# Queueing the weight casts of six gated-unit tiles behind a sigmoid, and two sets of operand combinations behind two low parts, in a bidirectional encoder layer

## The chip, the cores and the metric

The kernel runs on one core of one Trainium2 chip. The metric is the time of one execution on the device in microseconds; the figure given for a kernel is the median of its runs. The core has five engines with a queue of instructions each: TensorE (PE, matrix products into eight PSUM banks), the Vector engine (DVE), the Scalar engine (ACT), GpSimd (POOL) and SyncE (SP), which here issues most of the DMA transfers. An engine takes its instructions in the order of its queue; between engines, semaphores carry the dependences.

## What is computed

One layer of a hybrid encoder on 1024 positions of width 1024, in float32: a normalisation, one wide projection, two parallel mixers (a gated convolution module and a bidirectional linear recurrence), a merge, and a gated feed-forward block. The change touches only the beginning: the gated linear unit that feeds the convolution.

```python
h = _rmsnorm(x, attn_norm_w[layer])
proj = jnp.einsum("bsd,de->bse", h, w_in)
glu_in, q, v, z_f, z_b, og, g_a, g_b = jnp.split(proj, SPLIT_POINTS, axis=-1)
a = jax.nn.glu(glu_in, axis=-1)          # first half * sigmoid(second half), 512 columns each
a = _dwconv_centred(a, dw_w, dw_b)       # 31 taps over positions
```

## The kernel before

**Products in three parts.** Every operand of a product is split into a high part (a rounded copy, made by ACT) and a low part (source minus high part, made by DVE); `split` at L123 issues the two, both recorded at L124. `mm3` (L143) then makes one product of float32 accuracy from three matmuls: high by high (L148), high by low (L149), low by high (L150). PE's matmuls of one 128-column tile over 512 positions (one *half*) are 8 x 3 = 24.

**Tiles of the gated unit.** There are four column groups j, each with a *gate* tile (columns 512 + 128j) and a *value* tile (columns 128j), in two halves of 512 positions. `evac_b` (L848) takes a finished gate half out of its bank with a sigmoid (L851, on ACT) into a page of the tag "tm"; `evac_a` (L855) multiplies the value half by that page into `gl` (L857, on DVE). Both use the PSUM tag "mm", which has three banks. `glu_jobs` (L916) gives the order: a first job for j = 0, then first halves, both halves of j = 3, and last the second halves of gate 0, value 0, gate 1, value 1, gate 2, value 2. These are the "last six tiles" of the change.

**Preparing ahead.** `std_job` (L250) is a pair: `prep` loads the tile's 512 KB of raw weights (`raw_w`, L133, tag "wr", two pages, the DMA issued on SP at L135) and splits them into two of four "wp" pages; `run` issues the matmuls in pieces, four for a half. `run_jobs` (L194) calls the `prep` of a tile as the tile before it starts. A tile's weight pages are those of the tile two before it.

**Operand combinations.** After the gated unit the projections go through pairs of columns by a scheme with seven products instead of eight (`pair_job`, L282, first built as `pair0`). It needs differences of quadrants of h. `h_combos` (L937) loads three quadrants for each k = 0..3 into the tag "su" (four pages, L944 on SP), and `combos` (L461) makes three differences (L466, on DVE; the first of them into a "tm" page, of which there are four) and splits each into pages "hy" (L124 on ACT and DVE).

**What sets the order.** PE's order is written by hand: `Stream.fill(n)` advances the stream of the gated unit by n pieces, and `s_glu.fill(GLU_LATE)` with GLU_LATE = 17 stands behind the call of `h_combos` (L966, L967). PE does nothing in `h_combos`. The orders of ACT, DVE, POOL and SP are made when the program is built, by a scheduler that models the execution and ranks each instruction by how late it may be issued; the order in which instructions are traced in the program is one of its inputs. `tc.issue_after(i)` adds to this: what the block traces on the engine of `i` is issued behind `i`, without waiting for it to finish. Once built, an order is fixed.

After the gated unit the convolution follows (`conv_steps`, L1028): 31 steps on DVE for each j (L1036, L1039), with pieces of the pairs in between.

Of the kernel before, what the change touches and what calls it, by code (L numbers as in the profile page):

```python
# [10 lines left out]
F32 = mybir.dt.float32  # L11
# [3 lines left out]
AF = mybir.ActivationFunctionType  # L15
ALU = mybir.AluOpType
AX = mybir.AxisListType

P = 128
# [10 lines left out]
GLU_LATE = 17  # L30
# [17 lines left out]
def tile_hybrid_encoder(  # L48
# [24 lines left out]
    V, A, G, T = nc.vector, nc.scalar, nc.gpsimd, nc.tensor  # L73

    S, D = x.shape[1], x.shape[2]
    ND = D // P
    CW = conv_dw_w.shape[2]
# [16 lines left out]
    def nm(s):  # L94
        uid[0] += 1
        return f"{s}_{uid[0]}"
# [3 lines left out]
    def bank(tag):  # L100
        return ps.tile([P, H], F32, tag=tag, name=nm(tag), bufs=BANKS[tag])

    def page(pool, tag, bufs, dt=F32):
        return pool.tile([P, H], dt, tag=tag, name=nm(tag), bufs=bufs)

    def tmp():
        return page(mp, "tm", 4)
# [15 lines left out]
    def split(hi, lo, src, eng, late=False):  # L123
        parts = A.copy(hi, src), eng.tensor_tensor(lo, src, hi.bitcast(F32), op=ALU.subtract)  # L124
        if late:
            for i in parts:
                pin(i)
        return hi, lo

    def w_cols(w, r0, nk, c0, cols=P):  # L130
        return w[0, r0 : r0 + nk * P, c0 : c0 + cols].rearrange("(k p) e -> p k e", p=P)

    def raw_w(src, nk):  # L133
        t = mp.tile([P, nk, P], F32, tag="wr", name=nm("wr"), bufs=2)
        nc.sync.dma_start(t, src)  # L135
        return t

    def w_page(nk, pool=None):
        if pool is None:
            return mp.tile([P, nk, P], F32R, tag="wp", name=nm("wp"), bufs=4)  # L140
        return pool.tile([P, nk, P], F32R, tag="wq", name=nm("wq"), bufs=3)

    def mm3(acc, w, act, k, first, last, again=False):  # L143


        whi, wlo = w
        ahi, alo = act
        T.matmul(acc, whi[:, k, :], ahi, start=first, stop=False, skip_group_check=again)  # L148
        T.matmul(acc, whi[:, k, :], alo, start=False, stop=False, skip_group_check=again)  # L149
        T.matmul(acc, wlo[:, k, :], ahi, start=False, stop=last, skip_group_check=again)  # L150
# [43 lines left out]
    def run_jobs(jobs, lead=0, prime=0, first=None):  # L194


        live = collections.deque(maxlen=3)

        jobs = jobs if isinstance(jobs, collections.deque) else collections.deque(jobs)
        ready = collections.deque()  # L200

        def prepare(n):
            while jobs and len(ready) < n:
                prep, run = jobs.popleft()
                ready.append((run, prep()))
                live.append(ready[-1][1])

        def tick():
            for w in live:
                if isinstance(w, Weights):  # L210
                    w.tick()
            advance_chores()

        prepare(max(prime, 1))
        if prime:
            yield
        while ready:
            run, w = ready.popleft()
            pieces = run(w)
            for _ in itertools.islice(pieces, lead if first is None else first):  # L220
                tick()
                yield
            first = None
            prepare(1)
            for _ in pieces:
                tick()
                yield
            prepare(1)
# [21 lines left out]
    def std_job(src, nk, acts, evac, halves=(0, 1), step=2):  # L250


        def prep():
            raw = raw_w(src, nk)
            return split(w_page(nk), w_page(nk), raw, V)

        def run(w, halves=halves):
            for half in halves:
                acc = bank("mm")
                for k in range(nk):  # L260
                    mm3(acc, w, acts(k, half), k, k == 0, k == nk - 1)
                    if k % step == step - 1 or k == nk - 1:
                        yield
                evac(half, acc)

        return prep, run
# [194 lines left out]
    def combos(ops, k, b11, b12, b22, alloc):  # L461

        def sub(o, a, b):
            V.tensor_tensor(o, a, b, op=ALU.subtract)  # L466

        def parts(i, src):
            ops[i].append(split(alloc(), alloc(), src, V))

        t3 = page(mp, "tm", 4)
        sub(t3, b12, b22)
        parts(7, t3)
        sub(b22, t3, b11)
        parts(6, b22)
        sub(b12, b11, b12)
        parts(5, b12)
# [104 lines left out]
    def in_cols(c0):  # L582
        return w_cols(w_in, 0, ND, c0)
# [3 lines left out]
    ht = {i: [] for i in range(1, 8)}  # L587
# [256 lines left out]

    gate = {}
    early = []

    def evac_b(j):  # L848
        def evac(hf, acc):
            gate[j, hf] = tmp()  # L850
            A.activation(gate[j, hf], acc, AF.Sigmoid)  # L851

        return evac

    def evac_a(j):  # L855
        def evac(hf, acc):
            V.tensor_tensor(  # L857
                gl[j][:, PAD + hf * H : PAD + (hf + 1) * H], acc, gate.pop((j, hf)), op=ALU.mult
            )

        return evac

    def glu_tiles(j, halves):
        yield std_job(in_cols(CW + j * P), ND, h_std, evac_b(j), halves)
        yield std_job(in_cols(j * P), ND, h_std, evac_a(j), halves)

    glu_raw, glu_w = [], []

# [6 lines left out]
    def glu_first():  # L875


        def prep():
            for _ in range(2):
                glu_raw.append(mp.tile([P, ND, P], F32, tag="wr", name=nm("wr"), bufs=2))  # L880
                glu_w.append((w_page(ND), w_page(ND)))
            for g in range(2):
                ks = slice(g * NK2, (g + 1) * NK2)
                for c, raw in zip((CW, 0), glu_raw):
                    nc.sync.dma_start(raw[:, ks], in_cols(c)[:, ks])

        def run(_):
            accs = [bank("mm"), bank("mm")]
            seen = [0, 0]

            def mm(n, k, wp, ap):
                w, a = glu_w[n][wp][:, k, :], h_std(k, 0)[ap]
                seen[n] += 1
                T.matmul(accs[n], w, a, start=seen[n] == 1, stop=seen[n] == 3 * ND)


            mm(0, 0, 0, 0)
            mm(0, 0, 1, 0)
            yield
            mm(0, 1, 0, 0)  # L900
            mm(0, 1, 1, 0)
            for n, wp, ap in ((0, 0, 1), (1, 0, 0), (1, 0, 1), (1, 1, 0)):
                for k in range(2):
                    mm(n, k, wp, ap)
            yield
            for k in range(2, ND):
                for n in range(2):
                    for wp, ap in ((0, 0), (1, 0), (0, 1)):
                        mm(n, k, wp, ap)
                yield  # L910
            evac_b(0)(0, accs[0])
            evac_a(0)(0, accs[1])

        return prep, run

    def glu_jobs():  # L916
        def loaded(job, key, pages):
            def prep():
                return split(pages(), pages(), early[key], V)

            return prep, job[1]

        def early_page():
            return p0.tile([P, ND, P], F32R, tag="xn", name=nm("wp"), bufs=4)

        yield glu_first()
        job0, job1 = glu_tiles(1, (0,))
        yield loaded(job0, 0, early_page)
        yield loaded(job1, 1, lambda: w_page(ND))
        job0, job1 = glu_tiles(2, (0,))  # L930
        yield loaded(job0, 2, lambda: w_page(ND))
        yield job1
        yield from glu_tiles(3, (0, 1))
        for j in (0, 1, 2):
            yield from glu_tiles(j, (1,))

    def h_combos():  # L937
        def hy():
            return page(p1, "hy", 24, F32R)

        for k in range(NK2):
            b11, b12, b22 = (page(p1, "su", 4) for _ in range(3))
            for t, (kk, half) in ((b11, (k, 0)), (b12, (k, 1)), (b22, (k + NK2, 1))):
                nc.sync.dma_start(t, d_h[kk][half])  # L944
            combos(ht, k, b11, b12, b22, hy)

    s_glu = Stream(run_jobs(glu_jobs(), prime=1, first=GLU_LEAD))
    s_glu.fill()
    ahead = p0.tile([P, ND, P], F32, name="ahead")
# [13 lines left out]
    s_glu.fill(GLU_MORE)  # L963
    p0.release()
    p1 = tc.alloc_tile_pool(name="p1", bufs=1, reuse_waits="tile")
    h_combos()  # L966
    s_glu.fill(GLU_LATE)  # L967
    pair0 = in_pair(0)
    w_pair0 = pair0[0]()
    s_glu.drain()  # L970
# [737 lines left out]
    for k in range(NK2):  # L1708
        s_out.fill(16 if k else 17) if k < NK2 - 1 else s_out.drain()
        b11, b12, b21, b22 = x2[k][0], x2[k][1], x2[k + NK2][0], x2[k + NK2][1]  # L1710
# [358 lines left out]
```

## Time and profile before

| | |
|---|---|
| median of 3 runs | 1721.52 us (1721.14 to 1722.52) |
| the profiled execution | 1721.94 us, span 1720.0 us |
| PE busy | 99% of the span |
| DVE, ACT, POOL busy | 73%, 48%, 14% |
| mean granted PE clock | 0.998 |

In a row of a timeline stand the start in the span, the length in us, the engine, the line in the kernel, the operation with output and inputs, shapes and how many instructions are merged; in brackets the idle time of that engine before it, and what ended it. PE rows are matmuls whose ends are modelled, so the distance between starts says more than the lengths. "SPq" rows are the issue of transfers. In a view by windows stand the stretch, then for PE, weight loads (PEld), DVE, ACT and POOL the busy time and the count, then the granted PE clock, the share of the DMA engines and GB/s. A row of waits gives who waited for whom, the total, the number of times and the longest.

### The profile page before, as it was taken

Reading aid. Unit: us, or ns where it says so; the run is one execution under the profiler, and the core shown is the slowest. Engines: PE = TensorE matmul, PEld = TensorE weight load, DVE = VectorE, ACT = ScalarE, POOL = GpSimd, SP = SyncE. Lnnn points to the kernel's source line nnn. Section 1 sums busy time; section 2 is a strip of 40 time slices with the busy share of each in tenths; the row PEclk is TensorE's granted clock in tenths of the full one; section 3 lists DMA queues with packets and bytes.
Section 4 is the critical chain, followed back from the end, with each engine's and each line's share of the span. In section 5 each row is a group of like instructions: output and inputs, shape, how many; then the busy total and the mean of one; then the engine's idle time right before and its main releaser. Section 6 shows DMA issues by size and latency. Waiting matters only on the chain.

```text
span 1720.0 us, 30762 instructions
## 1 busy us (share of the span) xinstructions
PE 1699.1 (99%) x11902; PEld 1416.2 (82%) x11902; DVE 1256.6 (73%) x1937; ACT 825.0 (48%) x1544; POOL 240.7 (14%) x281
## 2 busy tenths in 40 slices
PE   8999999999999999999999999999999999999998
PEld 6878888788788888888888888888888888888787
DVE  4599999745779888888656466667777776657865
ACT  6443443233577777776442245444434433542334
POOL 1212222200001111111100002122222222000110
PEclk9999999999999999999999999999999999999999
DMA  8777888854673444435689466577778776783842
GB/s 281 238 181 177 201 191 189 203 160 148 202 261 91 146 127 133 128 116 200 223 277 279 143 205 199 147 159 153 165 166 174 171 172 154 229 266 102 215 95 99
DMA packets 337096, 308.28 MB, mean 179 GB/s; under 512 B 17582, under 2 KB 249142, under 8 KB 336950
## 3 DMA queue, kind: packets, MB, share of 16 engines
q1 hardware_dynamic: 289590, 267.51, 49.1%
q0 software_dynamic: 47360, 38.81, 15.5%
q8 instruction: 93, 1.52, 0.4%
q14 instruction: 53, 0.43, 0.1%
HBM read 201.40 MB, written 87.03 MB: 168 GB/s over the span
## 4 chain that ended last, share of the span: by engine, by line
PE 61%; DVE 1%; ACT 1%; DMA 0%; issue 0%; POOLq 0%; ACTq 0%; SPq 0%; DVEq 0%
PE mm L148 14%; PE mm L150 14%; PE mm L149 14%; PE sc L148 3%; PE sc L150 3%; PE sc L149 3%; PE ob L1375 2%; PE tr L148 1%; PE tr L150 1%; PE tr L149 1%; PE sc L1197 1%; PE sc L1283 1%; PE mm L1334 1%; PE sc L1334 1%; PE ob L1197 0%
## 5 line engine op out<-in xcount | busy, mean ns | idle before, releaser
L148 PE MATMUL mm<-hx,wp 128*128 128x512 f32 x1068 | 426.9, 400 | 2.3 <-ACT tm L851 1.4
L150 PE MATMUL mm<-hx,wp 128*128 128x512 f32 x1068 | 416.9, 390 | 0.5 <-DVE wp L124 0.5
L149 PE MATMUL mm<-hx,wp 128*128 128x512 f32 x1068 | 416.2, 390 | 0.0
L124 ACT CAST wp<-wr 128x1024 fp32r<-128x1024 f32 (+2 forms) x147 | 147.3, 1003 | 217.8 <-PE mm L149 180.3
L148 PEld LDWEIGHTS mm<-hx,wp 128*128 128x128 f32 x1068 | 200.6, 188 | 45.0 <-DVE ev L800 2.2
L150 PEld LDWEIGHTS mm<-hx,wp 128*128 128x128 f32 x1068 | 200.5, 188 | 44.4 <-DVE wp L124 1.6
L149 PEld LDWEIGHTS mm<-hx,wp 128*128 128x128 f32 x1068 | 200.8, 188 | 39.2 <-issue 0.7
L124 DVE TENSOR_TENSOR wp<-wr,wp 128x1024 fp32r<-128x1024 f32 (+2 forms) x145 | 169.1, 1167 | 39.1 <-ACT wp L124 32.7
L1039 DVE SCALAR_TENSOR_TENSOR acc<-gl,v_b,acc 128x1024 f32<-128x1024 f32 x120 | 148.7, 1272 | 0.4
L440 ACT COPY su<-mm 128x512 f32<-128x512 f32 x82 | 47.7, 582 | 80.1 <-PE mm L150 80.1
L1315 POOL DMA_DIRECT2D S<-D x64 | 36.3, 573 | 284.2 <-ACT S L1313 155.6
L1144 DVE TENSOR_TENSOR qF<-qF,tb 128x512 f32<-128x512 f32 x96 | 65.5, 684 | 13.3 <-ACT A L1178 12.7
L124 ACT CAST wq<-sw 128x1024 fp32r<-128x1024 f32 x41 | 43.2, 1053 | 61.2 <-PE mm L149 32.9
L148 PE MATMUL tr<-hx,wp 128*128 128x512 f32 x180 | 70.5, 392 | 0.0
L150 PE MATMUL tr<-hx,wp 128*128 128x512 f32 x180 | 70.1, 389 | 0.0
L149 PE MATMUL tr<-hx,wp 128*128 128x512 f32 x180 | 70.0, 389 | 0.0
L1144 DVE TENSOR_TENSOR kG<-kG,tb 128x512 f32<-128x512 f32 x96 | 65.5, 685 | 4.7 <-ACT A L1178 2.5
L1652 DVE SCALAR_TENSOR_TENSOR tm<-gp,v_a,tm 128x512 f32<-128x512 f32 x88 | 66.0, 750 | 4.0 <-ACT tm L1650 2.0
L301 POOL DMA_DIRECT2D sw<-in_ffn_w_up_dram x38 | 49.8, 1498 | 116.5 <-DMA sw<-in_ffn_w_up_dram 76.7
L148 PE MATMUL mm<-hy,wp 128*128 128x512 f32 x164 | 64.2, 391 | 0.0
L148 PE MATMUL sc<-hy,wq 128*128 128x512 f32 x164 | 64.2, 391 | 0.0
L150 PE MATMUL sc<-hy,wq 128*128 128x512 f32 x164 | 63.8, 389 | 0.0
(375 smaller groups left out, 3723.3 us busy)
## 6 DMA issues: line engine op xcount, KB each, us to landing
wr<-in_w_in_dram SPq DMA_DIRECT2D x48, 512.0 KB, 5.0
wr<-in_ffn_w_up_dram SPq DMA_DIRECT2D x22, 512.0 KB, 5.1
sw<-in_w_in_dram SPq DMA_DIRECT2D x38, 256.0 KB
d_g<-ft SPq DMA_DIRECT2D x38, 256.0 KB, 2.0
sw<-in_ffn_w_up_dram SPq DMA_DIRECT2D x38, 256.0 KB, 3.5
sw<-in_ffn_w_up_dram POOLq DMA_DIRECT2D x38, 256.0 KB, 6.2
wr<-sw POOLq DMA_DIRECT2D x32, 256.0 KB, 3.3
wr<-wr POOLq DMA_DIRECT2D x32, 256.0 KB, 3.4
```

The costliest lines, as they stand in the source:

```text
L124: parts = A.copy(hi, src), eng.tensor_tensor(lo, src, hi.bitcast(F32), op=ALU.subtract)
L148: T.matmul(acc, whi[:, k, :], ahi, start=first, stop=False, skip_group_check=again)
L149: T.matmul(acc, whi[:, k, :], alo, start=False, stop=False, skip_group_check=again)
L150: T.matmul(acc, wlo[:, k, :], ahi, start=False, stop=last, skip_group_check=again)
L301: G.dma_start(o, a, accum_op=ALU.add)
L440: A.copy(t, acc)
L1039: V.scalar_tensor_tensor(acc, g[:, k : k + S], tap(k), acc, op0=ALU.mult, op1=ALU.add)
L1144: return V.tensor_tensor(o, a, b, op=op)
L1315: G.dma_start(S_t[g : g + 32, :, g : g + 32], D_t[g : g + 32])
L1334: T.matmul(u[:, sl], kTs[d][:, sl], v[:, c, :], start=True, stop=True)
L1375: T.matmul(o[:, sl], l, r, start=(n == 0), stop=(n == len(terms) - 1))
L1652: V.scalar_tensor_tensor(c, g[:, o + k : o + k + H], vec("fdw", k * NF + j), c, op0=ALU.mult, op1=ALU.add,)
```

## The change

`evac_b` keeps the latest sigmoid in `last_gate`. The `prep` of each of the last six tiles is traced inside `issue_after` of that sigmoid, so that its cast on ACT is queued behind it. For value 1 and gate 2, `kept_lo` does the same work as `prep` and also keeps the subtraction that makes the low part. The combinations of k = 2 are traced inside `issue_after` of value 1's low part, those of k = 3 behind gate 2's; to have these, `h_combos` advances the stream by as many pieces as it takes, and these are taken off the 17 that follow.

```diff
     def evac_b(j):
         def evac(hf, acc):
             gate[j, hf] = tmp()
-            A.activation(gate[j, hf], acc, AF.Sigmoid)
+            last_gate[:] = [A.activation(gate[j, hf], acc, AF.Sigmoid)]
...
+    def behind_gate(job):
+        def prep():
+            with tc.issue_after(last_gate[0].ins):
+                return job[0]()
+
+        return prep, job[1]
+
+    def kept_lo(src, job):
+        def prep():
+            raw, hi, lo = raw_w(src, ND), w_page(ND), w_page(ND)
+            A.copy(hi, raw)
+            last_lo.append(V.tensor_tensor(lo, raw, hi.bitcast(F32), op=ALU.subtract))
+            return hi, lo
+
+        return prep, job[1]
...
         yield from glu_tiles(3, (0, 1))
         for j in (0, 1, 2):
-            yield from glu_tiles(j, (1,))
+            job0, job1 = glu_tiles(j, (1,))
+            yield behind_gate(kept_lo(in_cols(CW + j * P), job0) if j == 2 else job0)
+            yield behind_gate(kept_lo(in_cols(j * P), job1) if j == 1 else job1)
...
-            combos(ht, k, b11, b12, b22, hy)
+            if k >= 2:
+                while len(last_lo) < k - 1:
+                    s_glu.fill()
+                    fills.append(k)
+                with tc.issue_after(last_lo[k - 2].ins):
+                    combos(ht, k, b11, b12, b22, hy)
+            else:
+                combos(ht, k, b11, b12, b22, hy)
...
+    fills = []
     h_combos()
-    s_glu.fill(GLU_LATE)
+    s_glu.fill(GLU_LATE - len(fills))
```

More of the change, by code (lines that the diff above doesn't have):

```diff
@@ L846, in tile_hybrid_encoder @@
     early = []
+    last_gate, last_lo = [], []
     def evac_b(j):
```

## The prediction

> **What bounds the kernel now.** I read the page's busy times first, then who TensorE (PE) waited for over the whole span, then the stretches around the change, then each queue there.
>
> ```profile
> span 1720.0 us, 30762 instructions
> PE 1699.1 (99%) x11902; PEld 1416.2 (82%) x11902; DVE 1256.6 (73%) x1937; ACT 825.0 (48%) x1544; POOL 240.7 (14%) x281
> ```
> ```profile
> PE mm L148 <- ACT tm L851: 1.4, 1, 1.4
> ```
> ```profile
> 0.00:40.00 40.00, 33.51 (x154) 26.81 (x155) 19.91 (x33) 28.26 (x49) 7.72 (x24) 1.00 0.90 297
> 80.00:120.00 40.00, 38.55 (x170) 31.38 (x169) 38.38 (x53) 19.54 (x27) 5.44 (x9) 1.00 0.68 190
> 120.00:160.00 40.00, 40.00 (x178) 33.11 (x177) 40.00 (x53) 17.70 (x25) 9.43 (x9) 1.00 0.83 184
> 280.00:320.00 40.00, 39.30 (x174) 32.23 (x173) 39.64 (x38) 12.58 (x17) 9.26 (x9) 1.00 0.82 198
> 1680.00:1720.00 40.00, 31.75 (x252) 30.38 (x250) 20.20 (x52) 17.39 (x96) 2.42 (x3) 0.93 0.27 106
> ```
>
> PE is the bound: it is idle 1720.0 - 1699.1 = 20.9 us, of which 40 - 33.51 = 6.5 us lie at the start and 40 - 31.75 = 8.2 us at the end, where the change does not reach. That leaves 6.2 us in the whole middle of the program. One piece of it, 40 - 38.55 = 1.45 us, lies in the stage that the change touches, and the wait is named: a matmul waits for a sigmoid (L851). The shape of that wait on PE:
>
> ```profile
> 79.91 0.39 PE L148 MATMUL mm<-hx,wp 128*128 128x512 f32 x1
> 85.12 0.39 PE L150 MATMUL mm<-hx,wp 128*128 128x512 f32 x1
> 85.35 0.39 PE L148 MATMUL mm<-hx,wp 128*128 128x512 f32 x1
> 90.79 0.39 PE L148 MATMUL mm<-hx,wp 128*128 128x512 f32 x1
> 96.00 0.39 PE L150 MATMUL mm<-hx,wp 128*128 128x512 f32 x1
> 97.84 0.50 PE L148 MATMUL mm<-hx,wp 128*128 128x512 f32 x1 [1.45 <-ACT tm L851]
> 103.43 0.39 PE L148 MATMUL mm<-hx,wp 128*128 128x512 f32 x1
> 109.02 0.39 PE L148 MATMUL mm<-hx,wp 128*128 128x512 f32 x1
> 119.90 0.39 PE L148 MATMUL mm<-hy,wp 128*128 128x512 f32 x1
> ```
>
> A tile half is 24 matmuls. From 79.91 to 85.35 and on to 90.79 is 5.44 us each, 0.2267 us a matmul. So 79.91 starts gate 0, 85.35 value 0, 90.79 gate 1, 97.84 value 1, 103.43 gate 2, 109.02 value 2 (second halves), and 119.90 is the first product of the pair that uses the operand combinations. Value 1 should have started at 96.00 + 0.23 = 96.23: 1.61 us are lost. It and gate 2 then take 5.59 us each, 0.15 us above the others. There are three "mm" banks, so value 1 takes over the bank that gate 0 left, whose last matmul began at 85.12. Why was it not free? The Scalar engine's (ACT) queue says so, and the Vector engine's (DVE) beside it:
>
> ```profile
> 68.38 1.05 ACT L124 CAST wp<-wr 128x1024 fp32r<-128x1024 f32 x1 [3.30 <-PE mm L149]
> 74.20 0.60 ACT L851 ACTIVATE tm<-mm 128x512 f32<-128x512 f32 x1 [4.76 <-PE ob L519]
> 85.43 1.05 ACT L124 CAST wp<-wr 128x1024 fp32r<-128x1024 f32 x1
> 90.80 1.05 ACT L124 CAST wp<-wr 128x1024 fp32r<-128x1024 f32 x1 [3.28 <-PE mm L149]
> 95.51 0.62 ACT L124 CAST hy<-su 128x512 fp32r<-128x512 f32 x1 [0.58 <-DVE su L466]
> 96.24 1.04 ACT L124 CAST wp<-wr 128x1024 fp32r<-128x1024 f32 x1
> 97.19 1.08 ACT L851 ACTIVATE tm<-mm 128x512 f32<-128x512 f32 x2
> ```
> ```profile
> 69.47 1.22 DVE L124 TENSOR_TENSOR wp<-wr,wp 128x1024 fp32r<-128x1024 f32 x1 [5.53 <-ACT wp L124]
> 77.65 1.28 DVE L124 TENSOR_TENSOR hy<-su,hy 128x512 fp32r<-128x512 f32 x2
> 80.11 0.69 DVE L857 TENSOR_TENSOR gl<-mm,tm 128x512 f32<-128x512 f32 x1 [1.18 <-PE mm L150]
> 82.45 1.22 DVE L124 TENSOR_TENSOR wp<-wr,wp 128x1024 fp32r<-128x1024 f32 x1
> 83.59 0.69 DVE L124 TENSOR_TENSOR hy<-tm,hy 128x512 fp32r<-128x512 f32 x1
> 91.78 0.69 DVE L466 TENSOR_TENSOR tm<-su,su 128x512 f32<-128x512 f32 x1 [1.50 <-DMA su<-d_h]
> 94.19 0.69 DVE L124 TENSOR_TENSOR hy<-tm,hy 128x512 fp32r<-128x512 f32 x1
> 95.99 1.22 DVE L124 TENSOR_TENSOR wp<-wr,wp 128x1024 fp32r<-128x1024 f32 x1
> 99.01 0.69 DVE L466 TENSOR_TENSOR tm<-su,su 128x512 f32<-128x512 f32 x1
> 102.62 1.22 DVE L124 TENSOR_TENSOR wp<-wr,wp 128x1024 fp32r<-128x1024 f32 x1
> 117.55 1.22 DVE L124 TENSOR_TENSOR wp<-wr,wp 128x1024 fp32r<-128x1024 f32 x1
> ```
>
> Gate 0's last matmul ends at 85.12 + 0.39 = 85.51, but its sigmoid stands in the queue behind the combination cast at 95.51 and the weight cast of gate 2 at 96.24, and runs in a pair with gate 1's at 97.19. On DVE the low part of value 1 (95.99 to 97.21) stands behind the combinations of k = 2, which began at 91.78 only when a load had landed, though its high part was there at 90.80 + 1.05 = 91.85.
>
> **The change part by part.** Nothing is computed more or less: it moves issue order on two queues, and the order in which work is traced. PE's order, written by hand, stays: the 9 + 4 steps taken inside the combinations are taken off the 17 that followed.
>
> *The casts behind the sigmoids.* Each of the six casts must now issue after the latest sigmoid traced.
> - Gate 1's cast (85.43) goes behind gate 0's sigmoid: 85.6 to 86.2, cast to about 87.2, against 90.79 when it is needed. ACT idles 3.28 us just before 90.80, which hides the 0.8 us. The sigmoid now frees its bank at 86.2, ten microseconds early.
> - Gate 2's cast (96.24) goes behind gate 1's sigmoid: from 96.5, the cast ends near 98.2, its low part can follow to 99.4. Gate 2 will start at 96.23 + 5.44 = 101.7. Covered by 2.3 us.
> - Gate 0's cast (68.38) goes behind the sigmoid at 74.20, which itself waits for PE's transposes (L519): cast 74.80 to 75.85, where it is needed at 79.91. Its low part, 69.47 before, comes at 75.9 at the best, and at the worst behind the combinations of k = 0, at 77.65 + 1.28 = 78.9, ending at 80.15; the third matmul of gate 0 wants it at 79.91 + 0.45 = 80.36. Cost 0; DVE's idle 1.18 us before 80.11 takes its 1.22 us. Without that cover, one more value evacuation (0.69) in front would cost 0.5 us.
> - Value 0, 1 and 2 are pinned behind sigmoids already done by the time of their casts: nothing.
>
> *The combinations behind the low parts.* Value 1's low part goes ahead of k = 2: 91.85 to 93.1 in place of 95.99, and is wanted at 96.68. Were only the sigmoid moved, the old 97.21 would still stop value 1 for 0.53 us, so this half of the change is worth that much. k = 2 then starts at 93.1 instead of 91.78, and DVE's 1.50 us idle there can take a convolution step. Gate 2's low part (102.62 to 103.84, wanted at 103.88) goes ahead of k = 3 to about 99.4. k = 3 ran from 99.01 before and now starts about there. The combinations are first read at 119.90, some 16 us later. Hidden.
>
> *Loads.* The weight loads of the moved tiles keep their two raw pages, so the load that waits for gate 0's low part slips with it:
>
> ```profile
> 70.72 0.38 SPq L135 DMA_DIRECT2D wr<-in_w_in_dram  x1
> 72.44 2.98 SPq L378 DMA_DIRECT2D sw<-in_w_in_dram  x1
> 77.15 2.13 SPq L944 DMA_DIRECT2D su<-d_h  x3
> wr<-in_w_in_dram SPq DMA_DIRECT2D x48, 512.0 KB, 5.0
> ```
>
> From 70.72 to 77.1 at the best, 80.2 at the worst; with 5.0 us to landing, 82 to 85, and the cast of gate 1 wants it at 86.2. Cost 0, cover 1 us at the worst. The loads of value 2 and the first pair come earlier, since value 1's and gate 2's raw pages come free earlier.
>
> *The sum.* 1.61 us for the wait, 0.15 for value 1's slow restart, 0 to 0.15 for gate 2's third matmul, which met its low part 0.04 us before it was wanted; off it, 0 to 0.1 for the pair's product at 119.90, whose low weights end at 117.55 + 1.22 = 118.77 and would be wanted at 118.65 if nothing on DVE moved up. I take **1.7 us**, from bounds of 0 (all given back later) and 1.9. Profiled: 1721.94 with a span of 1720.0, so 1720.2 with a span of 1718.3. The three runs' median is 0.4 us below that execution: 1721.52 - 1.7 = **1719.8 us**. That is 0.1%; a change under 0.2% (3.4 us) is about what a measurement of this kernel cannot tell from none.
>
> **The rivals.**
>
> *Given back in the convolution stretch.* DVE is busy 40.00 of 40 us from 120 to 160, and the next PE wait has it as releaser:
>
> ```profile
> 303.03 0.50 PE L148 MATMUL mm<-hx,wp 128*128 128x512 f32 x1 [0.70 <-DVE ev L800]
> ```
>
> If DVE does not get ahead by what PE gains, that 0.70 becomes up to 2.4 us and the time stays at 1721.5. Against: DVE too had idle time before the stretch, 1.50 us at 91.78, that the new order can fill. 15%.
>
> *The sigmoid stands at the head of ACT and waits for its page.* This is the one that ends slower. The sigmoid writes one of four "tm" pages, shared with the combinations' first difference. If gate 0's sigmoid has its page only after k = 2's last reader, 94.19 + 0.69 = 94.88, then gate 1's cast, now behind it, ends at 94.9 + 0.6 + 1.0 = 96.5 where 90.79 was wanted: 5.7 us of wait, less the 1.7 = +4.0, 1725.5 us. It decides from a page that comes free after 90.79 - 1.05 - 0.60 = 89.1. For it: ACT idled before 90.80 and still did not take the ready sigmoid. Against: an engine's order is fixed when the program is built, so the idling proves no page wait, and with k = 2 pinned behind value 1, k = 1's difference is the last holder, free at 83.59 + 0.69 = 84.3. 8%.
> The Trainium skill, "TensorE: Matmul & The Clock Gate", Part 1 (the HAM clock gate), says that PE's clock drops to half after an idle window of about 3.4 us and needs as long a busy one to come back. By it this rival would cost an estimated 1.7 us more, 1727.2; no run here shows a middle wait that long, and the granted clock is 1.00 in the stretch with the 1.45 us wait.
>
> *The slipped load holds up SP.* If SP has gate 1's load ahead of the pair's loads and k = 1's, it stands there until 77.1 to 80.2, so all that followed 70.72, k = 1's loads last, is 6.4 to 9.5 us late. Value 0's low part (82.45), queued behind k = 1 on DVE, then ends at 90.1 to 93.2 where the third matmul of value 0 wants it at 85.80: 4.3 to 7.4 us, less the 1.7 = +2.6 to +5.7, 1724.1 to 1727.2. It decides from 2.1 us of lateness. Against: an issue order by readiness puts the pair's loads, whose pages are free at 71, first. 8%, half of it over 0.2%.
>
> *A new order everywhere.* The build re-plans all queues but PE's. The 6.2 - 1.45 = 4.7 us of other middle waits could shrink or grow: 1716.5 to 1719 where they shrink. 12%, half of it beyond -3.4 us.
>
> **How the numbers follow.** My forecast has 57%, given back 15, page 8, SP 8, re-planned 12. Faster by over 0.2%: half of the last, 0.06. Slower: the page and half of SP, 0.12. Within: 0.82. The forecast's own range is 1719.2 to 1720.8. The range for 8 in 10 takes in the given-back case with 1.5 us of scatter and the nearer half of the re-planned: 57 + 15 + 6 = 78, 1718.0 to 1723.0.
>
> **What would show it.** In the waits of PE, no wait of L148 for L851 and seven tile starts 5.44 us apart from 79.9 to 112.6. On ACT a sigmoid ahead of gate 1's cast near 85.6, and one ahead of gate 2's near 96.5. On DVE value 1's low part near 91.9, ahead of k = 2. At the pair's first "hy" product, 118.2 instead of 119.90; at 303.03, the wait still about 0.7 and at 301.3. I am wrong if PE waits for a weight cast at 79.9, 85.3 or 90.8, if the product with "hy" starts early and 303 does not, or if the time moves by more than 3.4 us.

## The result, and the profile after

The changed kernel takes 1724.68 us (median of 14 runs, 1723.10 to 1726.59) against 1722.40 us for the kernel before beside it: a ratio of 1.0016, 95% interval 1.0009 to 1.0023. It is slower by some 2.3 us where 1.7 us less was forecast, and outside the range of 1718.0 to 1723.0. The kernel before itself took 0.9 us more here than the 1721.52 us that the forecast started from; with the range moved by as much, up to 1723.9, the time is still outside. The profiled execution took 1726.39 us, 1.7 us above its own median, so I compare places in the two profiles and not their ends. In the changed kernel L851 has become L852 (sigmoid), L944 L963, L1036 and L1039 L1063 and L1066; `kept_lo` is L878 and L879.

The page's busy times, and who PE waited for between 20 and 345 us of the changed kernel:

```profile
PE 1700.2 (99%) x11902; PEld 1414.7 (82%) x11902; DVE 1257.5 (73%) x1937; ACT 824.7 (48%) x1544; POOL 241.1 (14%) x281
```
```profile
PE mm L148 <- DVE ev L800: 3.7, 4, 1.6
PE mm L150 <- DVE wp L124: 0.8, 1, 0.8
```

The wait for the sigmoid is gone. In its place stand four waits for an evacuation (L800), where there was one of 0.70 us, and one for a low part. The same by windows of PE alone, before and then after (stretch, length, busy time and count, granted clock, DMA share, GB/s):

```profile
70.00:120.00 50.00, 48.55 (x214) 1.00 0.74 208
120.00:200.00 80.00, 80.00 (x355) 1.00 0.84 190
200.00:345.00 145.00, 144.11 (x634) 1.00 0.82 192
```
```profile
70.00:120.00 50.00, 49.23 (x215) 1.00 0.77 213
120.00:200.00 80.00, 78.12 (x341) 1.00 0.81 180
200.00:345.00 145.00, 143.07 (x630) 1.00 0.83 193
```

PE's idle time is length minus busy: 1.45 + 0 + 0.89 = 2.34 us before, 0.77 + 1.88 + 1.93 = 4.58 us after. The difference of 2.24 us is about that of the medians (2.28). Where it arose, from PE's timeline of the changed kernel:

```profile
79.06 0.39 PE L148 MATMUL mm<-hx,wp 128*128 128x512 f32 x1
100.82 0.39 PE L148 MATMUL mm<-hx,wp 128*128 128x512 f32 x1
107.88 0.50 PE L150 MATMUL mm<-hx,wp 128*128 128x512 f32 x1 [0.77 <-DVE wp L124]
118.57 0.50 PE L148 MATMUL mm<-hy,wp 128*128 128x512 f32 x1
130.31 0.50 PE L148 MATMUL mm<-hx,wp 128*128 128x512 f32 x1 [0.52 <-DVE ev L800]
170.33 0.50 PE L148 MATMUL mm<-hx,wp 128*128 128x512 f32 x1 [1.25 <-DVE ev L800]
304.58 0.50 PE L148 MATMUL mm<-hx,wp 128*128 128x512 f32 x1 [0.34 <-DVE ev L800]
325.55 0.50 PE L148 MATMUL mm<-hx,wp 128*128 128x512 f32 x1 [1.59 <-DVE ev L800]
```

From the start of gate 0 (79.06) to that of gate 2 (100.82) are 21.76 us, four halves of 5.44. Before, it was 103.43 - 79.91 = 23.52. So 1.76 us were won, the forecast amount. The first "hy" product at 118.57 is 1.33 us ahead of 119.90, but 0.85 of that the changed kernel already had at 79.06. This is not the change's doing: e3 and e11 (below), which do not have it, start gate 0 at 78.77 and 78.79. So 0.48 us are left there: the rest was lost between 100.82 and 118.57, 0.77 of it at 107.88. At 304.58 it is 1.55 us behind 303.03.

**The early loss.** ACT, then DVE, of the changed kernel:

```profile
73.84 1.05 ACT L124 CAST wp<-wr 128x1024 fp32r<-128x1024 f32 x1
85.08 0.59 ACT L852 ACTIVATE tm<-mm 128x512 f32<-128x512 f32 x1
85.57 1.04 ACT L124 CAST wp<-wr 128x1024 fp32r<-128x1024 f32 x1
95.91 0.59 ACT L852 ACTIVATE tm<-mm 128x512 f32<-128x512 f32 x1
```
```profile
74.34 0.68 DVE L466 TENSOR_TENSOR tm<-su,su 128x512 f32<-128x512 f32 x1
74.94 1.22 DVE L124 TENSOR_TENSOR wp<-wr,wp 128x1024 fp32r<-128x1024 f32 x1
...
80.64 0.69 DVE L124 TENSOR_TENSOR hy<-su,hy 128x512 fp32r<-128x512 f32 x1 [0.34 <-ACT hy L124]
...
91.70 1.21 DVE L879 TENSOR_TENSOR wp<-wr,wp 128x1024 fp32r<-128x1024 f32 x1
94.66 0.69 DVE L466 TENSOR_TENSOR tm<-su,su 128x512 f32<-128x512 f32 x1 [1.74 <-DMA su<-d_h]
...
103.00 0.68 DVE L466 TENSOR_TENSOR tm<-su,su 128x512 f32<-128x512 f32 x1
...
106.61 1.22 DVE L124 TENSOR_TENSOR wp<-wr,wp 128x1024 fp32r<-128x1024 f32 x1
```

The sigmoids stand where they were meant to, at 85.08 and 95.91, each ahead of a cast. But gate 0's cast now comes at 73.84 instead of 68.38, and its low part (74.94) stands in the middle of k = 0's combinations. They end at 80.64 + 0.69 = 81.33, before at 77.65 + 1.28 = 78.93. The "su" pages come free later, the loads for k = 1 and k = 2 go out later, DVE stands 1.74 us at k = 2 (94.66), k = 3 starts at 103.00, and value 2's low part behind it comes at 106.61. Its reader on PE waits 0.77 us for it, until 107.88. Gate 2's low part, forecast for 99.4, is held up as well: it ends at 100.06 + 1.22 = 101.28, just when PE wants it; in e14 and e8 PE waits 0.23 and 0.56 us for it.

**The later loss.** A pair computes products 1, 2, 6, 7, 5, 4, 3. Products 1, 6, 5 and 3 add up in one "mm" bank, and between 5 and 3 DVE must subtract that bank from product 7 (`evac(1, 1, p7, row, ALU.subtract)`, run at L800). Meanwhile PE has only product 4, 12 matmuls or 2.72 us. DVE, at the pairs near 168 and 322 us before, and at those near 168, 303 and 324 us after (L1039 and L1066 are convolution steps, L1078 adds up outputs of the convolution that were loaded back; "wq<-sw" is the low part of the *next* pair's column sums):

```profile
167.75 0.67 DVE L800 TENSOR_TENSOR ev<-su,mm 128x512 f32<-128x512 f32 x1
168.35 1.21 DVE L124 TENSOR_TENSOR wq<-sw,wq 128x1024 fp32r<-128x1024 f32 x1
169.48 1.27 DVE L1039 SCALAR_TENSOR_TENSOR acc<-gl,v_b,acc 128x1024 f32<-128x1024 f32 x1
...
320.59 1.23 DVE L124 TENSOR_TENSOR wq<-sw,wq 128x1024 fp32r<-128x1024 f32 x1 [0.24 <-ACT wq L124]
321.73 0.68 DVE L800 TENSOR_TENSOR ev<-su,mm 128x512 f32<-128x512 f32 x1
```
```profile
167.25 1.23 DVE L124 TENSOR_TENSOR wq<-sw,wq 128x1024 fp32r<-128x1024 f32 x1 [0.34 <-ACT wq L124]
168.40 1.28 DVE L1066 SCALAR_TENSOR_TENSOR acc<-gl,v_b,acc 128x1024 f32<-128x1024 f32 x1
169.59 0.68 DVE L800 TENSOR_TENSOR ev<-su,mm 128x512 f32<-128x512 f32 x1
...
303.24 0.69 DVE L1078 TENSOR_TENSOR tm<-cx 128x512 f32<-128x512 f32 x1 [1.13 <-DMA cx<-d_cv]
303.85 0.68 DVE L800 TENSOR_TENSOR ev<-su,mm 128x512 f32<-128x512 f32 x1
...
323.68 1.22 DVE L124 TENSOR_TENSOR wq<-sw,wq 128x1024 fp32r<-128x1024 f32 x1
324.81 0.68 DVE L800 TENSOR_TENSOR ev<-su,mm 128x512 f32<-128x512 f32 x1
```

Near 168 us the same three instructions stand in another order: evacuation, low part, step before; low part, step, evacuation after. PE waits 1.25 us at 170.33 for it. Near 130 us the low part (128.44) also stands ahead of the evacuation (129.58) now, where before the evacuation (129.84) was ahead of the low part (130.43); PE waits 0.52 us at 130.31.

Farther on, these two did not change places that way. Near 303 us the low part was ahead before (301.16, then the evacuation at 302.29), where PE waited its 0.70 us; after, the evacuation is ahead, but behind an instruction that waits 1.13 us for its load, and PE waits 0.34 us. Near 324 us the low part is ahead in both kernels. There DVE comes to it 3.09 us later (323.68 against 320.59) and PE to product 4 only 1.60 us later (321.08 against 319.48). So the 1.59 us at 325.55 go with a DVE that has fallen behind PE: from 120 to 320 us it is idle for 200 - 195.97 = 4.03 us, 1.13 of them at 303.24; before, it was idle for 200 - 198.70 = 1.30 us.

### The profile page after: what moved, and what is told of

The parts are those of the page before. It is cut to its first block, busy times and chain, and to the rows that moved or that the text cites. A ratio compares the mean times of both kernels' runs of the same rounds, so it can differ in the third digit from the quotient of the medians.

```text
span 1724.4 us, 30751 instructions
## 1 busy us (share of the span) xinstructions
PE 1700.2 (99%) x11902; PEld 1414.7 (82%) x11902; DVE 1257.5 (73%) x1937; ACT 824.7 (48%) x1544; POOL 241.1 (14%) x281
## 4 chain that ended last, share of the span: by engine, by line
PE 53%; DVE 2%; DMA 1%; issue 1%; ACT 0%; POOLq 0%; ACTq 0%; SPq 0%; DVEq 0%
PE mm L148 12%; PE mm L150 12%; PE mm L149 12%; PE sc L148 3%; PE sc L150 3%; PE sc L149 3%; PE tr L148 1%; PE tr L150 1%; PE tr L149 1%; PE ob L1402 1%; DVE hx L124 0%; DMA wr<-in_ffn_w_down_dram 0%; DMA tm<-d_gc 0%; PE sc L1939 0%; PE sc L1224 0%
## 5 line engine op out<-in xcount | busy, mean ns | idle before, releaser
L150 PE MATMUL mm<-hx,wp 128*128 128x512 f32 x1068 | 417.1, 391 | 1.3 <-DVE wp L124 1.3
L124 ACT CAST wp<-wr 128x1024 fp32r<-128x1024 f32 (+2 forms) x145 | 145.1, 1001 | 206.2 <-PE mm L149 166.3
L150 PEld LDWEIGHTS mm<-hx,wp 128*128 128x128 f32 x1068 | 200.4, 188 | 46.0 <-DVE wp L124 2.6
L124 DVE TENSOR_TENSOR wp<-wr,wp 128x1024 fp32r<-128x1024 f32 (+2 forms) x143 | 166.8, 1167 | 34.7 <-ACT wp L124 28.5
L1066 DVE SCALAR_TENSOR_TENSOR acc<-gl,v_b,acc 128x1024 f32<-128x1024 f32 x120 | 148.9, 1277 | 0.4
L124 ACT CAST wq<-sw 128x1024 fp32r<-128x1024 f32 x41 | 43.2, 1053 | 60.2 <-PE mm L149 32.9
L150 PE MATMUL tr<-hx,wp 128*128 128x512 f32 x180 | 70.1, 389 | 0.0
L148 PE MATMUL mm<-hy,wp 128*128 128x512 f32 x164 | 64.3, 392 | 0.0
L148 PE MATMUL sc<-hy,wq 128*128 128x512 f32 x164 | 64.2, 391 | 0.0
L149 PE MATMUL mm<-hy,wp 128*128 128x512 f32 x164 | 63.8, 389 | 0.0
```

The costliest lines, as they stand in the source:

```text
L1066: V.scalar_tensor_tensor(acc, g[:, k : k + S], tap(k), acc, op0=ALU.mult, op1=ALU.add)
```

## The experiments

Times are medians; the ratio to the kernel before in the same session has its 95% interval. "Idle" is PE's idle time in the three windows above (length minus busy) in the profile of that kernel.

| run | us | ratio | idle 70-120 | 120-200 | 200-345 |
|---|---|---|---|---|---|
| the change | 1724.68 | 1.0016 [1.0009, 1.0023] | 0.77 | 1.88 | 1.93 |
| e14, the change again | 1725.87 | 1.0018 [1.0009, 1.0027] | 1.03 | 1.91 | 1.61 |
| e1, casts only | 1744.92 | 1.0128 [1.0111, 1.0146] | 14.07 | 0.12 | 4.09 |
| e2, combinations only | 1723.14 | 1.0002 [0.9993, 1.0011] | 0 | 1.38 | 1.78 |
| e5, without gate 0, value 0 | 1724.05 | 1.0004 [0.9995, 1.0013] | 0 | 1.37 | 2.08 |
| e6, gate 0, value 0 only | 1725.69 | 1.0018 [1.0009, 1.0027] | 0.80 | 1.91 | 1.71 |
| e13, gate 0's low part later | 1724.74 | 1.0010 [1.0001, 1.0019] | 1.12 | 0.66 | 2.14 |
| e3, fewer steps, before | 1723.84 | 1.0006 [0.9997, 1.0015] | 1.45 | 1.34 | 0 |
| e4, fewer steps, changed | 1723.57 | 1.0001 [0.9992, 1.0009] | 1.13 | 0.58 | 0.28 |
| e7, e2 + evacuation first | 1720.24 | 0.9985 [0.9976, 0.9994] | 0 | 0 | 0.55 |
| e8, change + evacuation first | 1720.59 | 0.9984 [0.9976, 0.9993] | 1.37 | 0 | 0.15 |
| e12, e5 + evacuation first | 1720.00 | 0.9982 [0.9974, 0.9991] | 0 | 0 | 0.66 |
| e11, before + evacuation first | 1722.82 | 0.9999 [0.9990, 1.0008] | 1.61 | 0 | 1.68 |
| e9, before, other page | 1728.33 | 1.0040 [1.0027, 1.0053] | 1.79 | 0.05 | 2.79 |
| e10, e1, other page | 1725.72 | 1.0020 [1.0011, 1.0029] | 1.50 | 1.87 | 1.62 |

**The two halves apart.** e1 has only the casts, with the combinations traced as before; e2 has only the combinations.

```diff
 e1, h_combos:
-            if k >= 2:
...
-                with tc.issue_after(last_lo[k - 2].ins):
-                    combos(ht, k, b11, b12, b22, hy)
...
+            combos(ht, k, b11, b12, b22, hy)
 e2, glu_jobs:
-            yield behind_gate(kept_lo(in_cols(CW + j * P), job0) if j == 2 else job0)
-            yield behind_gate(kept_lo(in_cols(j * P), job1) if j == 1 else job1)
+            yield kept_lo(in_cols(CW + j * P), job0) if j == 2 else job0
+            yield kept_lo(in_cols(j * P), job1) if j == 1 else job1
```

> Only the six casts are queued behind the latest sigmoid; the combinations are traced and ordered as before. Theory A (DVE is the late engine from about 95 us to 325 us, so the 1.6 us that PE wins at value 1 is given back at the evacuations of the convolution stretch, and re-planned orders there cost more): PE does not wait for the sigmoid at value 1, but the sum of PE's waits for L800 between 100 and 350 us grows from 0.7 us to 1.5 us or more; time within 1 us of before. Rival B (the pins of the combinations alone do the harm, by pushing the combinations back): L800 waits stay near 0.7 us and the time is 1 to 1.7 us below before.

> Only the combinations of k = 2 and 3 are moved (traced in between the tiles and queued behind the low parts); no cast is queued behind a sigmoid. The DVE order of the convolution stretch is that of the changed kernel. Theory A, with the order of that stretch as the price: the L800 waits are about those of the changed kernel (3 to 4 us in sum) and the time is 1.5 to 3 us above before. Rival (the casts behind the sigmoids, gate 0's low part above all, do the harm): L800 waits near 0.7 us, time at or below before.

The casts alone cost 22.4 us, where both expectations had it within 2 us of before. PE's waits from 20 to 345 us, and ACT, in e1:

```profile
PE mm L148 <- ACT wp L124: 8.4, 1, 8.4
PE mm L150 <- DVE wp L124: 5.6, 1, 5.6
```
```profile
95.25 1.22 ACT L124 CAST hy<-su 128x512 fp32r<-128x512 f32 x2 [1.78 <-DVE su L466]
96.38 0.59 ACT L852 ACTIVATE tm<-mm 128x512 f32<-128x512 f32 x1
96.87 1.03 ACT L124 CAST wp<-wr 128x1024 fp32r<-128x1024 f32 x1
```

Gate 0's sigmoid was planned behind the casts of k = 2, and gate 1's cast behind that sigmoid, at 96.87. PE stood for it 8.4 us. The combinations alone, in e2, win all that the change could win in this part: PE has no idle time from 70 to 120 us, and the sigmoid runs at 85.43 with no pin. So the pins on the casts add nothing to the gain, and without the other half they do the harm of the rival with the page. The L800 waits (3.0 us in three) come with e2 too; its time, 0.6 us above before, is under the 1.5 to 3 us expected, and its interval does not tell it from before.

**Which pin makes the early loss.** e5 leaves the first two tiles unpinned, e6 pins only these; e13 keeps the change whole and queues gate 0's low part behind the last low part of k = 0 (an edge that orders DVE's queue and adds no wait).

```diff
 e5:  +  pin0 = behind_gate if j else lambda job: job
 e6:  +  pin0 = (lambda job: job) if j else behind_gate
 both: yield pin0(...) in place of yield behind_gate(...)
 e13, behind combos(...) of k == 0:
+                    tc.add_manual_dep(
+                        gate0_low[0].ins,
+                        last_split[0].ins.name,
...
```

> The changed kernel without the queueing of gate 0's and value 0's casts; the four later casts stay behind their sigmoids, the combinations behind the low parts. Theory A2 (gate 0's cast, moved from 68 us behind the sigmoid at 74 us, puts its low part into the chain of the combinations and costs the 2.3 us that the changed kernel loses between 103 and 150 us; the two evacuations placed behind a low part at about 168 and 323 us cost another 2.8 us): no early loss, both L800 waits stay, time as with the combinations alone, 0 to 1 us above before. Rival (a later cast, gate 2's, makes the early loss): PE waits near 101 and 107 us stay, time 1.5 to 3 us above before.

> The complement: of the six casts only gate 0's and value 0's are queued behind a sigmoid, with the combinations as in the changed kernel. Theory A2: all of the loss, PE waits near 107 and 130 us and both L800 waits, time 1.5 to 3 us above before. Rival: time 0 to 1 us above before.

> The changed kernel with all its pins, and one edge more: gate 0's low part queued on the Vector engine behind the combinations of k = 0, in place of in the middle of them. Theory (the early loss comes from that low part holding up the chain that frees the pages for the loads of k = 1 and k = 2, not from the late cast itself): the low part ends near 79.3, still ahead of the matmul that wants it near 80.4, the loads of k = 2 are issued about 2 us earlier, the Vector engine does not idle for them, and PE has no wait from 70 to 120 us. The Vector engine's new order has the evacuation ahead of the low part at the second pair, so the wait of 1.25 us near 168 should go too; time 1 to 3 us under the changed kernel. Rival (the cast behind the sigmoid is itself too late): a PE wait of 0.3 us or more for a weight at 79 to 81 us, and at most 0.7 us won.

> The changed kernel as it is, beside the run above on one chip. Its waits from 70 to 120 us (0.8) and for the evacuation (about 3.7) should come back as they were if they belong to the issue order and not to one execution; time +1.5 to +4 us against before.

Every kernel with gate 0's pin has 0.77 us or more of idle time from 70 to 120 us (the change, e14, e6, e8, e13); those with the combinations moved and without that pin have none (e2, e5, e7, e12). Here is SP, then DVE, in e5; in the changed kernel the loads of k = 2 went out later:

```profile
84.57 2.08 SPq L964 DMA_DIRECT2D su<-d_h  x2
88.64 0.68 SPq L964 DMA_DIRECT2D su<-d_h  x1
```
```profile
92.31 0.69 DVE L466 TENSOR_TENSOR tm<-su,su 128x512 f32<-128x512 f32 x1
```
```profile
86.95 0.34 SPq L963 DMA_DIRECT2D su<-d_h  x1
88.69 1.66 SPq L963 DMA_DIRECT2D su<-d_h  x2
```

In e5, k = 2 starts at 92.31 without a wait, 2.35 us ahead of 94.66. In e13 the expectation failed in its main point: the rival's wait at 80 us is there. PE, then DVE (L125 and L152 are L124 and L150 there):

```profile
80.19 0.50 PE L152 MATMUL mm<-hx,wp 128*128 128x512 f32 x1 [0.85 <-DVE wp L125]
```
```profile
78.92 1.22 DVE L125 TENSOR_TENSOR wp<-wr,wp 128x1024 fp32r<-128x1024 f32 x1
```

Behind the combinations, at 78.92, the low part is too late for its own matmul (0.85 us). Ahead of them it makes k = 2 and value 2 late (0.77). Neither of the two places is harmless. That no place would be is not shown: a sum of 1.22 us for a later pair (77.18) stood ahead of the low part in e13 as well. e13 is 1.1 us under the change beside it (e14), with intervals that overlap. The wait near 170 did go, but not for the reason expected: the low part still stands ahead of the evacuation (167.34, then 168.49), only the convolution step between them is gone. In time, this pin costs 0.8 us (the change against e5) to 2.5 us (e6 against e2) by the medians' distances from the kernel before, with intervals that overlap. Side by side on one chip, e6 takes 1.6 us more than e5 (95% interval of the difference of the medians, by resampling the runs, 0.8 to 2.9), so of the pins the first two are the ones that cost. They are gate 0's and value 0's; value 0's cast hardly moves (79.03 in the change, 78.94 in e5), so I put the cost down to gate 0's. With the evacuation first (e8, e12) it cannot be seen.

**Load or order.** e3 and e4 leave out every second step of the convolution (15 of 31 for each j), in the kernel before and in the changed one.

```diff
             for k in range(1, CK):
+                if k % 2 == 0:
+                    yield
+                    continue
```

> The kernel before with every second tap of the convolution left out (15 of 31 steps for each of the four column groups, some 71 us of DVE work less between 100 and 330 us). Theory A: DVE has idle time in the stretch, no L800 wait there, the sigmoid wait of about 1.45 us stays; time 0.5 to 1.5 us below before. Rival: the L800 wait at 303 us does not depend on DVE's load, time as before.

> The changed kernel with the same taps left out. Theory A: without the full DVE the win at value 1 stays, no L800 waits, so it is 1 to 1.9 us below the shortened kernel before. Rival (the loss comes from something other than DVE's load, the later loads or the new order everywhere): it is 1 to 3 us above the shortened kernel before.

A lighter DVE does not help the kernel before, which was expected to gain 0.5 to 1.5 us: it still loses the 1.45 us for the sigmoid, and gets an L800 wait of 1.34 us at 169.41 that it did not have, where the new plan has the low part (167.53) ahead of the evacuation (168.66). Up to there DVE is still full (40.00 of 40 us busy from 120 to 160). Later it is not (12.81 of 40 us from 240 to 280), and the wait at 303 us is gone. In the changed kernel (e4) the L800 waits fall from 3.7 to 0.8 us, those near 170, 303 and 324 us are gone, and the early loss stays; it is 0.3 us under e3, between the two expectations. So the waits near 303 and 324 us do not come with a DVE that has time to spare, and the one near 168 us follows the order. Leaving out steps also makes a new plan, so these two runs alone do not part load from order.

**The evacuation first.** One edge: the low part of the next pair's column sums is queued behind the evacuation of this pair's bank. On e2 (e7), the change (e8), the kernel before (e11) and e5 (e12).

```diff
             evac(1, 1, p7, row, ALU.subtract)
+            for low in column_lows:
+                tc.add_manual_dep(
+                    low.ins,
+                    last_evac[0].ins.name,
...
```

> The combinations moved, no cast queued, and in the pairs of the convolution stretch the low part of the next pair's column sums is queued behind the evacuation that frees the bank of the last product (a queueing edge alone, no computation changed). Theory A2 with the issue order as the price: the L800 waits at 168 and 323 us (1.25 and 1.59 us) go, the 1.6 us won at value 1 stays, time 1 to 2.5 us below before. Rival A (DVE's load, not its order, makes these waits): they come back elsewhere in the stretch and the time is 0 to 1 us above before.

> The changed kernel with the same queueing of the low parts behind the evacuations. Theory A2: the waits at 168 and 323 us go and the early loss of about 2.3 us stays, time 0 to 1 us above before. Rival A: the waits come back elsewhere, 1.5 to 3 us above before.

> The kernel before with one edit: the low part of the next pair's column sums queued behind the evacuation that frees the pair's bank. Theory (the gain of that edge is the removal of an L800 wait that the order of the Vector engine made): the kernel before has one such wait, 0.70 us at 303, so this gains at most 0.7 us: -0.9 to +0.5 us; the sigmoid's 1.45 us stays. Rival (the edge shortens the program by itself, at all pairs, whatever the change): -2 us or more.

> The changed kernel without the pins of gate 0's and value 0's casts, and with the evacuation ahead of the next low part. Theory (two separate losses: gate 0's cast behind its sigmoid, about 1.5 us, and the L800 waits, about 3 us): both are gone, -2 to -3.5 us against before, at least as fast as the combinations-only kernel with that edge (-2.5), and 0.5 to 1.5 us under the changed kernel with that edge. Rival (the pin of gate 0 costs nothing once the evacuation is early): same as the changed kernel with that edge, -2 us within 0.4.

DVE in e7 (L814 is L800 there):

```profile
164.19 0.68 DVE L814 TENSOR_TENSOR ev<-su,mm 128x512 f32<-128x512 f32 x1
164.79 1.22 DVE L125 TENSOR_TENSOR wq<-sw,wq 128x1024 fp32r<-128x1024 f32 x1
```

The waits near 168 and 324 us are gone, and the time falls by 2.4, 2.0 and 2.6 us under the kernel before (e7, e8, e12); these three beat both kernels and cannot be told from one another. For e8, 0 to 1 us above before was expected: its early idle time of 1.37 us stays, yet it cannot be told from e7 on the same chip (0.35 us apart, interval by resampling -0.6 to 1.6). In e12 the interval (0.9974 to 0.9991) does not exclude its rival, so that gate 0's pin costs time once the evacuation is early is not shown. On the kernel before (e11) the edge gains nothing: the wait at 303 goes, the sigmoid's 1.61 us stays, and one of 1.68 us for L800 appears at 341.26, behind an instruction that waited for its load (339.19). So the edge pays only together with the moved combinations, and only with it does their gain reach the end. It takes away the wait near 168 us, where the order had changed, and the one near 324 us, where DVE was late: there the evacuation no longer has the 1.22 us of the low part ahead of it.

**The page.** In e9 (the kernel before) and e10 (e1) the first difference of the combinations goes to an "ev" page, which leaves the four "tm" pages to others.

```diff
-        t3 = page(mp, "tm", 4)
+        t3 = ev()
```

> The kernel before with one edit: the first difference of the combinations is written to an "ev" page instead of a "tm" page, so that only sigmoids use the "tm" pages. Theory (the sigmoid of gate 0 ran late at 97.19 because its page was held by the combinations of k = 2): the sigmoid runs near 86, PE has no wait for it (the 1.45 us at 97.84 goes), and, since the queues are re-planned as in the other variants, 1 to 3 us of waits for the evacuation (L800) appear near 168 to 325: time -1 to +1.5 us against before. Rival (the page did not matter, the planner set the cast ahead of the sigmoid for its own reason): the sigmoid stays behind the cast of gate 2, the wait of 1.45 us stays, time within 0.5 us.

> The six casts queued behind sigmoids, the combinations traced as before (as in the run that lost 22 us), and the first difference in an "ev" page. Theory (those 22 us came from the sigmoid at the head of the Scalar engine's queue waiting for a "tm" page that the combinations hold): the waits of 8.4 and 5.6 us go, time like the changed kernel, +1 to +3 us against before. Rival (the casts of the combinations ahead of it, not the page, hold the sigmoid): a PE wait of over 4 us for a weight cast near 91 stays, +10 us or more.

ACT in e9:

```profile
85.85 0.59 ACT L851 ACTIVATE tm<-mm 128x512 f32<-128x512 f32 x1
```

The sigmoid comes at 85.85 instead of 97.19 by this edit alone, and in e10 the 8.4 us wait is gone and the time is that of the changed kernel. So the page that it shares with the combinations is what put the sigmoid late, in the kernel before and in e1. e9 is slower than expected (+5.8 us, not -1 to +1.5): value 1's low part still stands behind k = 2 and now costs 1.79 us at 97.89, where the prediction had put 0.53 on that half; and at 305.04 PE waits 2.58 us, because DVE stood 4.24 us for a load at the head of its queue. It is the load that made DVE stand 1.13 us in the change; e2, e5, e6, e10, e13 and e14 have this stop too, with 0.99 to 1.82 us.

## Why the prediction was wrong

- **The gain** was right in place and size: 1.76 us between gate 0 and gate 2, no wait for the sigmoid, the sigmoids at 85.08 and 95.91, value 1's low part at 91.70. The two halves do need each other, but not as I had it: the combinations alone do it all (e2), since with them out of the way the shared page comes free.
- **Gate 0's cast at cost 0** was the first step that failed. I asked whether its low part would meet its own reader, and left open on which side of k = 0's combinations it would stand. Ahead of them it holds up their pages, so the loads, so k = 2, k = 3 and value 2; I did not follow that chain. It took 0.77 us at 107.88 (1.28 us by 118.57). The other side, my worst case, came in e13: the low part ended at 80.14, forecast 80.15, and still cost 0.85 us. PE wanted it at 79.34 and not at 80.36, so the cover of 0.2 us, read from one execution, was not there.
- **DVE's 1.50 us of idle time at 91.78** were to take a convolution step. One more step (89.91) did move ahead of k = 2, but the load came later too, so 1.74 us were left idle; without gate 0's pin (e5) the step fills the time and DVE does not wait. And k = 3 started at 103.00, not 99.4.
- **Given back in the convolution stretch** had the right releaser, and was right that DVE is late near 303 and 324 us; its price was too low. I let DVE give back what PE gains and no more, so I capped the time at 1721.5. But DVE lost time of its own, idle for 4.03 us from 120 to 320 us in place of 1.30, and the L800 waits from 200 to 345 us rose from 0.70 to 1.93 us. Another 1.77 us came at 130.31 and 170.33, where there had been none: not given back, but a changed order.
- **A new order everywhere** was the second step that failed, and the one that decides: I priced only the waits that shrink, 1716.5 to 1719, and gave growth no figure. PE's idle time grew by 1.88 us from 120 to 200 us and by 1.04 us from 200 to 345 us, together more than the gain. What I had not asked is which waits stood one instruction away: at 167.75 the evacuation was just ahead of the low part, and product 4 covers only 2.72 us.
- **The other rivals.** The page rival did not come in the change, but it is real: e1 is that case, with 22.4 us where I had 4.0. The slipped load came at 76.19 and held nothing up, as forecast.

- **The size that can be told apart.** I held a change under 0.2% for one that a measurement cannot tell from none. The interval of 1.0009 to 1.0023 tells this one.

What stays open: why the plan sets the low part ahead of the evacuation. It did so near 168 us in the change, e2, e5, e6 and e13, but also in e10 and e3, where the combinations are not moved, so the cause is no single edit. Open too is how much of the 1.59 us near 324 us is the low part standing ahead and how much is DVE's lateness. The idle times account for the medians within 1.4 us, which is as much as some of the differences between runs, except where PE's clock fell (e1, e9).

## What to carry to other kernels

When a local edge makes the builder plan again, list the places where another engine's wait is near zero only because two neighbouring instructions stand in a good order, or because that engine arrives just in time, and price each for the bad order: the loss can be larger than the gain that the edit was made for. Pin the order that matters (here, the evacuation that frees a bank ahead of work for the next pair) together with the change, or the gain may not reach the end. When a producer is delayed, follow every chain on the engine it now shares, down to the pages that it frees and the loads that wait for them, not only its own reader.

## What the runs showed of the hardware

PE's clock fell to half after a shorter wait than I had expected. In e9 PE stood from 302.46 to 305.04 (2.96 us from the start of one matmul to the next); PE's rows after it, and one window behind (PE, PEld, DVE, ACT, POOL, clock, DMA share, GB/s):

```profile
305.04 0.50 PE L148 MATMUL mm<-hx,wp 128*128 128x512 f32 x1 [2.58 <-DVE ev L800]
...
306.12 0.63 PE L148 MATMUL mm<-hx,wp 128*128 128x512 f32 x1
306.54 0.63 PE L149 MATMUL mm<-hx,wp 128*128 128x512 f32 x1
...
309.02 0.40 PE L149 MATMUL mm<-hx,wp 128*128 128x512 f32 x1
```
```profile
306.00:308.00 2.00, 2.00 (x6) 1.51 (x6) 2.00 (x4) 0.00 (x0) 0.00 (x0) 0.50 0.48 155
```

The granted clock is 0.50, and matmuls start 0.42 us apart instead of 0.2267, until 309.02. The ten intervals from 305.04 take 3.98 us instead of 2.27: the wait costs another 1.7 us. The wait of 1.79 us in the same kernel had no such effect: the matmul behind it started 0.34 us later, the next 0.23. The Trainium skill, "TensorE: Matmul & The Clock Gate", Part 1 (the HAM clock gate), puts the fall behind an idle window of about 3.4 us; here 2.58 us were enough, and the measurement decides. In e1 the matmuls behind the waits of 5.63 us (104.81) and 3.87 us (301.35) start 0.43 us apart as well, and the granted clock is 0.50 from 97.95 to 104.36, behind the one of 8.44 us. Behind these three waits the intervals above 0.2267 us add up to 3.5 us. e1's profiled execution (1742.49 us) is 20.0 us above the kernel before's median and 2.4 us under its own; 15.9 us of added idle time and these 3.5 us account for 19.4 of the 20.0.
